# The left operands of the MLP's second half: one at a time through three products, with their sums on VectorE, instead of in packs of seven with their sums on GpSimd

## The chip, the cores and the metric

The kernel runs on one core of one Trainium2 chip. Five engines with queues of their own work side by side: TensorE (PE; PEld is its weight load), VectorE (DVE), ScalarE (ACT), GpSimd (POOL) and SyncE (SP), whose queue issues all transfers here. Each takes its instructions in order and waits for semaphores of the others. The metric is the device time of one execution in microseconds (us).

## The reference

One layer of a streaming encoder on 2048 positions with 1024 channels. A mixer (short convolution and retention) comes first; the change lies behind it, in the MLP:

```python
h = rms_norm(x, g_pre_mlp[layer]) * (1.0 + scale2) + shift2
f = jnp.square(jax.nn.relu(h @ w_fc1[layer])) @ w_fc2[layer]
x = x + gate2 * rms_norm(f, g_post_mlp[layer])
```

with `w_fc1` 1024 x 4096 and `w_fc2` 4096 x 1024, all in float32.

## The kernel before

**Products of three.** A float32 tile is split into a high part (ScalarE casts it to fp32r, line 806) and a low part (VectorE subtracts the high part from the tile, line 807). `mm3` makes one product from three matmuls (lines 142 to 144): high by high, low by high, high by low.

**Seven products for eight.** Each half of the positions (`B` = 0 and 1, 1024 positions) goes through both linear maps of the MLP by the Strassen-Winograd scheme: a 2x2 block product is made from seven products, numbered in the order 1, 2, 6, 7, 5, 3, 4, with sums of blocks on either side. The sequence is `fc1(0)`, `fc2(0)`, `fc1(1)`, `fc2(1)`.

**Left operands of fc1.** `h_left` makes them from the normalised activations in DRAM (`h2d`). For each of four packs p it loads four tiles a11, a12, a21, a22, makes four sums (s3 at line 842, and lines 847, 849, 851), and splits seven tiles (`sp_`), one per product. The splits stay in SBUF: qh and ql are their high and low parts. For B = 0 the work is done ahead of fc1(0). For B = 1 it is done beside fc2(0), with the engine for the sums handed over as `eng`.

**fc2 and its steps.** A product of fc2 is a loop over t = 0 to 15 (`prod`). Each step loads one tile `fw` of 128x1024, the activations (from `fd`) and the weights next to each other (line 964), splits both (fh and fl, wh and wl), and runs twelve matmuls, three for each of four PSUM banks. There are three buffers for fw, three each for wh and wl, ten for fh and fl together. So a load of fw for step t waits for wl of step t - 3, and a cast to wh waits for the matmuls of step t - 3.

**What sets the order.** The program is written in one sequence. A scheduler then places the instructions on each engine's queue, by priority and by its own model of times, so that work written later can stand earlier. `next(beside)` in `prod` says where in the written sequence a piece of `h_left` belongs.

Of the kernel before, what the change touches and what calls it, by code (L numbers as in the profile page):

```python
# [54 lines left out]
def block_kernel(  # L55
# [5 lines left out]
    nc = tc.nc  # L61
# [15 lines left out]
    def nm(s):  # L77
        n_of[s] = n_of.get(s, 0) + 1
        return f"{s}_{n_of[s]}"
# [108 lines left out]
    def mod1(kt):  # L188

        pt = st.tile([P, 256], F32, tag="pt", name=nm("pt"), bufs=4)  # L190
        for i in range(2):
            raw = st.tile([P, 4, 256], F32, tag="ada", name=nm("ada"), bufs=8)
            last = nc.sync.dma_start(raw, ada1[kt, i].rearrange("p (k c) -> p k c", k=4))
            for k in range(4):
                c_ = sc[:, 4 * i + k : 4 * i + k + 1]
                if i == k == 0:
                    nc.vector.tensor_scalar(pt, raw[:, k, :], c_, None, op0=ALU.mult)
                else:
                    nc.vector.scalar_tensor_tensor(  # L199
                        pt, raw[:, k, :], c_, pt, op0=ALU.mult, op1=ALU.add  # L200
                    )
        return pt, last
# [69 lines left out]
    with tc.tile_pool(name="st", bufs=NK) as st:  # L272
# [37 lines left out]
        pts, _ = mod1(0)  # L310
# [23 lines left out]
    def at(tag, shape=(P, 512), dt=F32, bufs=4):  # L334
        pool = {"yh": pl, "yl": pl, "kT": late, "sg": late}.get(tag, pa)
        return pool.tile(list(shape), dt, tag=tag, name=nm(tag), bufs=bufs)
# [156 lines left out]
    NP = DFF // P // 2  # L493
# [21 lines left out]
    with pa_stack:  # L515
# [30 lines left out]
        for b in range(NB):  # L546
# [36 lines left out]
            for ps in gemm_nat(w_in(GG), h_cur, KS):  # L583
                sg = at("sg")
# [5 lines left out]
            for t in range(NT):  # L590
# [3 lines left out]
                kT = at("kT")  # L594
# [195 lines left out]
    def q(n, tag):  # L790
        pool, t_ = late, tag
        if n % 2 == 0:
            pool, t_ = (pQ, tag) if tag == "junk" else (tp, {"kT": "tmpa", "sg": "tmpb"}[tag])
        return pool.tile([P, 512], F32, tag=t_, name=nm("q"), bufs=QB[tag])

    def r_():
        return h_("r", F32)

    def ld(src):
        a = r_()  # L800
        nc.sync.dma_start(a, src)
        return a

    def split512(src, tile_of):
        hi, lo = tile_of("h"), tile_of("l")
        nc.scalar.copy(hi, src)  # L806
        nc.vector.tensor_tensor(lo, src, hi.bitcast(F32), op=SUB)  # L807
        return hi, lo
# [10 lines left out]
    def left_tile(i):  # L819
        if i == 4:  # L820
            return lambda part: pQ.tile([P, 512], F32R, tag="four", name=nm("q" + part), bufs=8)
        return held(hA if i in (1, 2, 6) else hB)

    sd = {i: [dram.tile([P, 512], F32, name=f"sd{i}_{p}") for p in range(4)] for i in (7, 5, 3)}

    def h_left(B, res, eng, t2k, now):


        def sp_(i, a):
            if now or i not in sd:  # L830
                res[i].append(split512(a, left_tile(i)))
            else:
                nc.sync.dma_start(sd[i][len(sdn[i])], a)
                sdn[i].append(a)

        sdn = {i: [] for i in sd}
        for p in range(4):
            a11, a12, a21, a22 = (t2k(n) for n in range(4))
            for a, (i, j) in ((a11, (0, 0)), (a12, (0, 1)), (a21, (1, 0)), (a22, (1, 1))):
                nc.sync.dma_start(a, h2d[2 * B + i][2 * p + j])  # L840
            s3 = t2k(4)
            eng.tensor_tensor(s3, a11, a21, op=SUB)
            sp_(7, s3)
            sp_(1, a11)
            sp_(2, a12)
            sp_(4, a22)
            eng.tensor_tensor(a21, a21, a22, op=ADD)
            sp_(5, a21)
            eng.tensor_tensor(a11, a21, a11, op=SUB)
            sp_(6, a11)  # L850
            eng.tensor_tensor(a12, a12, a11, op=SUB)
            sp_(3, a12)
            yield
        if not now:
            for i in (7, 5, 3):
                for p in range(4):
                    res[i].append(split512(ld(sd[i][p]), left_tile(i)))
                yield

    def quads(t):  # L860
        return [ld(w1[t][:, i * 512 : i * 512 + 512]) for i in range(4)]
# [92 lines left out]
    def fc2(B, beside=None):  # L954
# [13 lines left out]

        def prod(i, bs, upto=NP, aside=None):
            for t in range(upto):  # L970
                if beside is not None and i in (1, 2) and t % 4 == 2:
                    next(beside, None)
                ah, al, bh, bl = operands(i, t)
                for n, ps in enumerate(bs):
                    s = slice(n * P, n * P + P)
                    mm3(ps, ah[:, s], al[:, s], bh, bl, t == 0, t == NP - 1)
                if aside is not None:
                    next(aside, None)
# [91 lines left out]

    hl = [{i: [] for i in ORDER} for _ in range(2)]
    left = h_left(0, hl[0], nc.vector, lambda n: r_(), False)
    for _ in range(4):
        next(left)
    fc1(0, hl[0], quads(0), left, mixer_end())
    tail = fc2(0, h_left(1, hl[1], nc.gpsimd, lambda n: q(1, "kT" if n < 4 else "sg"), True))
    fc1(1, hl[1], quads(0), None, tail)
    fc2(1)

# [83 lines left out]
```

## Time and profile before

| | us |
|---|---|
| median of 3 runs | 2254.37 (2247.35 to 2257.65) |
| the profiled execution | 2248.11 |
| its span, first to last instruction | 2246.30 |
| PE busy | 2146.0 (96%) |
| DVE busy | 1446.0 (64%) |
| ACT busy | 989.3 (44%) |
| POOL busy | 616.0 (27%) |

The page's chain of waits gives 64% of the span to PE, 12% to transfers, 7% to DVE and 5% to POOL. The busy shares are means over all stages. To see what one stage waits for, the span is cut into windows of time, and the rows of one engine are read in order of time with the idle time in front of each. A granted clock (PEclk) of 1.00 is TensorE's full 2.4 GHz.

### The profile page before, as it was taken

The numbers are of one execution on the slowest core, as the hardware profiler recorded it, in microseconds if no ns is written. First come the engines' busy times: TensorE is split into PE (matmuls) and PEld (weight loads), VectorE is DVE, ScalarE is ACT, GpSimd is POOL, SyncE is SP. The second block draws the span as 40 slices with busy tenths as digits, with TensorE's granted clock in tenths as the row PEclk, the third lists the DMA queues.
The fourth block names the chain that finished last, engine by engine and source line by source line (L and its number), as shares of the span: only waits on it lengthen the run. The fifth ranks groups of instructions, "written<-read, shape, count | busy, mean of one in ns | idle before, by whom it ended". The sixth has DMA issues, their size and how long they took to land.

```text
span 2246.3 us, 28437 instructions
## 1 busy us (share of the span) xinstructions
PE 2146.0 (96%) x9736; PEld 1769.4 (79%) x9736; DVE 1446.0 (64%) x2182; ACT 989.3 (44%) x1714; POOL 616.0 (27%) x457
## 2 busy tenths in 40 slices
PE   3999999999999999979999989999999999999997
PEld 2788877878787888868888867888888888888885
DVE  7766854774577535776666776656776666555566
ACT  3332533253224422565555554444445555454453
POOL 4133163305323442152333331101333333010012
PEclk8999999999999999999999999999999999999998
DMA  7456477446655563665444366666764443666656
GB/s 277 138 176 225 160 244 244 158 151 224 203 188 189 193 223 106 229 206 189 154 155 155 136 220 200 195 192 197 253 235 150 150 149 138 193 197 196 197 188 253
DMA packets 197426, 428.23 MB, mean 191 GB/s; under 512 B 22560, under 2 KB 22560, under 8 KB 197280
## 3 DMA queue, kind: packets, MB, share of 16 engines
q1 hardware_dynamic: 197280, 426.41, 57.5%
q8 instruction: 76, 1.25, 0.2%
q14 instruction: 70, 0.57, 0.1%
HBM read 322.51 MB, written 103.81 MB: 190 GB/s over the span
## 4 chain that ended last, share of the span: by engine, by line
PE 64%; DMA 12%; issue 11%; DVE 7%; POOL 5%; ACT 1%; SPq 1%; DVEq 0%; POOLq 0%; ACTq 0%
PE g L142 19%; PE g L144 19%; PE g L143 19%; DMA w2r<-in_w 3%; DMA w2d<-w2r 2%; POOL w2r L502 2%; PE m L142 2%; PE m L143 2%; PE m L144 2%; DMA ada<-in_ada 1%; DMA fw<-fd 1%; DMA x<-in_x 1%; DVE pt L199 1%; DVE ql L807 1%; DVE wl L807 1%
## 5 line engine op out<-in xcount | busy, mean ns | idle before, releaser
L143 PE MATMUL g<-ql,wh 128*128 128x512 f32 x896 | 350.0, 391 | 9.8 <-DVE ql L807 9.8
L144 PE MATMUL g<-qh,wl 128*128 128x512 f32 x896 | 350.2, 391 | 0.8 <-DVE wl L807 0.6
L142 PE MATMUL g<-qh,wh 128*128 128x512 f32 x896 | 349.4, 390 | 0.8 <-ACT wh L806 0.6
L136 ACT CAST whi<-raw 128x1024 fp32r<-128x1024 f32 x148 | 155.3, 1052 | 348.2 <-PE g L144 175.5
L864 DVE TENSOR_TENSOR q<-g,q 128x512 f32<-128x512 f32 x267 | 178.4, 687 | 174.3 <-PE g L144 174.1
L138 DVE TENSOR_TENSOR wlo<-raw,whi 128x1024 fp32r<-128x1024 f32 x140 | 188.9, 1353 | 151.1 <-ACT whi L136 150.7
L143 PE MATMUL g<-wl,fh 128*128 128x512 f32 x680 | 266.9, 392 | 8.9 <-DVE wl L807 8.8
L807 DVE TENSOR_TENSOR fl<-fw,fh 128x512 fp32r<-128x512 f32 x218 | 165.7, 761 | 170.1 <-ACT fh L806 168.9
L144 PE MATMUL g<-wh,fl 128*128 128x512 f32 x680 | 265.9, 391 | 0.0
L806 ACT CAST fh<-fw 128x512 fp32r<-128x512 f32 x218 | 135.2, 620 | 234.6 <-DMA fw<-fd 225.9
L806 ACT CAST wh<-r 128x512 fp32r<-128x512 f32 x224 | 138.8, 620 | 216.3 <-PE g L143 189.3
L142 PE MATMUL g<-wh,fh 128*128 128x512 f32 x680 | 219.8, 391 | 2.7 <-ACT wh L806 2.7
L143 PEld LDWEIGHTS g<-ql,wh 128*128 128x128 f32 x896 | 168.6, 188 | 46.2 <-DVE ql L807 11.6
L144 PEld LDWEIGHTS g<-qh,wl 128*128 128x128 f32 x896 | 168.7, 188 | 37.4 <-DVE wl L807 2.8
L142 PEld LDWEIGHTS g<-qh,wh 128*128 128x128 f32 x896 | 168.7, 188 | 36.5 <-ACT wh L806 0.8
L807 DVE TENSOR_TENSOR wl<-fw,wh 128x512 fp32r<-128x512 f32 x218 | 158.2, 727 | 45.4 <-ACT wh L806 45.1
L994 POOL TENSOR_TENSOR q<-q,gg 128x512 f32<-128x512 f32 x28 | 43.1, 1566 | 467.2 <-ACT q L991 342.0
L807 DVE TENSOR_TENSOR wl<-r,wh 128x512 fp32r<-128x512 f32 x224 | 164.1, 733 | 10.9 <-ACT wh L806 10.4
L806 ACT CAST wh<-fw 128x512 fp32r<-128x512 f32 x218 | 134.8, 619 | 65.5 <-PE g L144 31.3
L882 POOL TENSOR_TENSOR r<-r,r 128x512 f32<-128x512 f32 x32 | 42.4, 1325 | 429.0 <-DVE wl L807 388.8
L143 PEld LDWEIGHTS g<-wl,fh 128*128 128x128 f32 x680 | 128.5, 189 | 38.4 <-DVE wl L807 11.9
L142 PEld LDWEIGHTS g<-wh,fh 128*128 128x128 f32 x680 | 128.0, 189 | 30.5 <-ACT wh L806 3.9
(257 smaller groups left out, 4478.0 us busy)
## 6 DMA issues: line engine op xcount, KB each, us to landing
raw<-in_win SPq DMA_DIRECT2D x116, 512.0 KB, 4.2
fd<-q SPq DMA_DIRECT2D x224, 256.0 KB, 2.2
fw<-fd SPq DMA_DIRECT2D x224, 256.0 KB, 2.7
r<-in_w SPq DMA_DIRECT2D x128, 256.0 KB, 4.7
fw<-w2d SPq DMA_DIRECT2D x128, 256.0 KB, 3.0
ada<-in_ada SPq DMA_DIRECT2D x48, 512.0 KB, 4.7
fw<-in_w SPq DMA_DIRECT2D x96, 256.0 KB, 3.5
w2r<-in_w SPq DMA_DIRECT2D x32, 512.0 KB, 4.9
```

The costliest lines, as they stand in the source:

```text
L136: nc.scalar.copy(hi, raw)
L138: (eng or nc.vector).tensor_tensor(lo, raw, hi.bitcast(F32), op=ALU.subtract)
L142: nc.tensor.matmul(ps, ah, bh, start=first, stop=False)
L143: nc.tensor.matmul(ps, ah, bl, start=False, stop=False)
L144: nc.tensor.matmul(ps, al, bh, start=False, stop=last)
L199: nc.vector.scalar_tensor_tensor(pt, raw[:, k, :], c_, pt, op0=ALU.mult, op1=ALU.add)
L502: nc.gpsimd.tensor_tensor(o, a, b_, op=ALU.subtract)
L806: nc.scalar.copy(hi, src)
L807: nc.vector.tensor_tensor(lo, src, hi.bitcast(F32), op=SUB)
L864: (eng or nc.vector).tensor_tensor(o, a, b_, op=ADD)
L882: nc.gpsimd.tensor_tensor(b11, b12, b11, op=SUB)
L994: eng.tensor_tensor(c, c, gg[1][:, j * 512 : j * 512 + 512], op=ALU.mult)
```

## The change

For B = 1, `h_left` now hands back control after each split operand and no longer after a pack of seven. `prod` calls for the next one in products 1, 2 and 6, from the fifth step of product 1 on, 28 calls over 40 steps, where it called once every four steps of products 1 and 2. The sums of lines 842 to 851 (844 to 859 now) are made on VectorE (`nc.vector`) and no longer on GpSimd (`nc.gpsimd`). For B = 0 the 28 calls are made in one loop, as the four were.

```diff
+    LEFT = 28
+
     def h_left(B, res, eng, t2k, now):
...
             s3 = t2k(4)
             eng.tensor_tensor(s3, a11, a21, op=SUB)
             sp_(7, s3)
+            yield
             sp_(1, a11)
+            yield
             sp_(2, a12)
+            yield
             sp_(4, a22)
+            yield
             eng.tensor_tensor(a21, a21, a22, op=ADD)
             sp_(5, a21)
+            yield
             eng.tensor_tensor(a11, a21, a11, op=SUB)
             sp_(6, a11)
+            yield
             eng.tensor_tensor(a12, a12, a11, op=SUB)
             sp_(3, a12)
             yield
...
         def prod(i, bs, upto=NP, aside=None):
             for t in range(upto):
-                if beside is not None and i in (1, 2) and t % 4 == 2:
-                    next(beside, None)
+                if beside is not None and i in (1, 2, 6):
+
+                    k = (1, 2, 6).index(i) * NP + t - 4
+                    if k >= 0 and (k + 1) * LEFT // 40 > k * LEFT // 40:
+                        next(beside, None)
...
     left = h_left(0, hl[0], nc.vector, lambda n: r_(), False)
-    for _ in range(4):
+    for _ in range(LEFT):
         next(left)
     fc1(0, hl[0], quads(0), left, mixer_end())
-    tail = fc2(0, h_left(1, hl[1], nc.gpsimd, lambda n: q(1, "kT" if n < 4 else "sg"), True))
+    tail = fc2(0, h_left(1, hl[1], nc.vector, lambda n: q(1, "kT" if n < 4 else "sg"), True))
```

What the scheduler makes of it changes in one place of the program alone, steps 6 of product 1 to 8 of product 2 of fc2(0); ahead of it and behind it the kinds and the order of the instructions are the same on every engine. On VectorE, the first pack of left operands stood like this before (ql is a low part of a left operand, fl and wl those of the activations and weights of a step of fc2):

```order
L807 TENSOR_TENSOR ql_11328<-q_11325,qh_11327 128x512
L807 TENSOR_TENSOR fl_11518<-fw_11514,fh_11517 128x512
L807 TENSOR_TENSOR wl_11522<-fw_11514,wh_11521 128x512
L807 TENSOR_TENSOR ql_11345<-q_11319,qh_11344 128x512
L807 TENSOR_TENSOR fl_11541<-fw_11537,fh_11540 128x512
L807 TENSOR_TENSOR ql_11350<-q_11317,qh_11349 128x512
L807 TENSOR_TENSOR fl_11564<-fw_11560,fh_11563 128x512
L807 TENSOR_TENSOR wl_11545<-fw_11537,wh_11544 128x512
L807 TENSOR_TENSOR ql_11355<-q_11318,qh_11354 128x512
```

In the changed program the same pack stands like this, with the four sums (L844, L853, L856, L859) in VectorE's own queue:

```order
L807 TENSOR_TENSOR ql_11474<-q_11387,qh_11473 128x512
L844 TENSOR_TENSOR q_11394<-q_11386,q_11388 128x512
L807 TENSOR_TENSOR wl_11435<-fw_11427,wh_11434 128x512
L853 TENSOR_TENSOR q_11388<-q_11388,q_11389 128x512
L807 TENSOR_TENSOR ql_11501<-q_11389,qh_11500 128x512
L807 TENSOR_TENSOR ql_11397<-q_11394,qh_11396 128x512
L856 TENSOR_TENSOR q_11386<-q_11388,q_11386 128x512
L807 TENSOR_TENSOR fl_11454<-fw_11450,fh_11453 128x512
L807 TENSOR_TENSOR ql_11552<-q_11388,qh_11551 128x512
L807 TENSOR_TENSOR wl_11458<-fw_11450,wh_11457 128x512
L859 TENSOR_TENSOR q_11387<-q_11387,q_11386 128x512
L807 TENSOR_TENSOR fl_11481<-fw_11477,fh_11480 128x512
```

Sums and left splits now alternate with the splits of the steps. From the first left split to the last there were 55 VectorE rows (28 left splits, 14 fl, 13 wl); there are 80 now (28 left splits, 16 sums, 18 fl, 18 wl).

On SP, the loads of the second pack (q from h2d) stood between the loads of the steps (fw) like this before:

```order
L840 DMA q_11450<-h2d_2_639 128x512
L964 DMA fw_11624<-fd_1_10_8017 128x512
L964 DMA fw_11624<-in_w 128x512
L840 DMA q_11451<-h2d_3_640 128x512
L840 DMA q_11452<-h2d_2_647 128x512
L964 DMA fw_11647<-fd_1_11_8018 128x512
L964 DMA fw_11647<-in_w 128x512
L840 DMA q_11453<-h2d_3_648 128x512
```

and stand like this now:

```order
L842 DMA q_11657<-h2d_2_639 128x512
L842 DMA q_11658<-h2d_3_640 128x512
L972 DMA fw_11527<-fd_1_10_8017 128x512
L972 DMA fw_11527<-in_w 128x512
L842 DMA q_11659<-h2d_2_647 128x512
L972 DMA fw_11555<-fd_1_11_8018 128x512
L972 DMA fw_11555<-in_w 128x512
L842 DMA q_11660<-h2d_3_648 128x512
```

The second load has moved ahead of one step's loads; in the later packs each of the four stands by itself between the loads of two steps. Before, a load of h2d waited for a split on VectorE and, three times in four, for a sum on GpSimd; now it waits for a split on VectorE alone.

## Rows read from the trace of the kernel before

**Rows 1.** The page's first part, all engines: busy us, share of the span, instructions.

```profile
PE 2146.0 (96%) x9736; PEld 1769.4 (79%) x9736; DVE 1446.0 (64%) x2182; ACT 989.3 (44%) x1714; POOL 616.0 (27%) x457
```

**Rows 2.** Windows ahead of the stretch, of the stretch, and behind it: from:to, length, then busy us (instructions) of PE, PEld, DVE, ACT, POOL, then the granted clock, the share of the DMA engines and GB/s.

```profile
1270.00:1310.61 40.61, 40.61 (x180) 33.61 (x180) 29.31 (x42) 21.80 (x38) 6.54 (x4) 1.00 0.48 158
1310.61:1368.07 57.46, 46.45 (x182) 35.47 (x181) 47.56 (x57) 33.61 (x61) 25.05 (x16) 0.94 0.63 201
1380.00:1600.00 220.00, 220.00 (x972) 182.15 (x972) 134.58 (x200) 103.15 (x185) 21.81 (x16) 1.00 0.65 207
```

**Rows 3.** TensorE in order of time: start, us, what, and in brackets the idle time in front and what ended it. Line 142 is the first of the three matmuls and its first row the start of a step.

```profile
1310.61 0.61 PE L142 MATMUL g<-wh,fh 128*128 128x512 f32 x2
...
1313.33 0.61 PE L142 MATMUL g<-wh,fh 128*128 128x512 f32 x2
...
1316.05 1.07 PE L142 MATMUL g<-wh,fh 128*128 128x512 f32 x4
1319.16 0.80 PE L143 MATMUL g<-wl,fh 128*128 128x512 f32 x1 [2.04 <-DVE wl L807]
...
1321.04 0.63 PE L143 MATMUL g<-wl,fh 128*128 128x512 f32 x1
1321.46 0.63 PE L144 MATMUL g<-wh,fl 128*128 128x512 f32 x1
...
1368.07 0.62 PE L142 MATMUL g<-wh,fh 128*128 128x512 f32 x2
...
1371.41 0.73 PE L142 MATMUL g<-wh,fh 128*128 128x512 f32 x2 [0.46 <-ACT wh L806]
```

**Rows 4.** Windows of ten microseconds, columns as in rows 2.

```profile
1280.00:1290.00 10.00, 10.00 (x46) 8.27 (x45) 9.10 (x15) 5.28 (x9) 1.31 (x1) 1.00 0.36 134
...
1320.00:1330.00 10.00, 10.00 (x40) 8.12 (x40) 7.65 (x13) 4.61 (x8) 2.80 (x2) 0.88 0.79 244
1330.00:1340.00 10.00, 7.37 (x25) 5.28 (x24) 9.61 (x12) 5.78 (x11) 3.47 (x3) 0.83 0.66 208
```

**Rows 5.** Waits in the stretch 1310.61 to 1368.07 us: who waited for whom, us in all, times, longest.

```profile
ACT fh L806 <- DMA fw<-fd: 12.5, 5, 3.0
...
ACT qh L806 <- DMA q<-h2d: 9.7, 9, 1.9
PE g L143 <- DVE wl L807: 8.8, 5, 2.3
...
PE g L142 <- ACT wh L806: 2.2, 2, 1.7
```

**Rows 6.** GpSimd in order of time: the four sums of the first pack, and the last of the third.

```profile
1311.63 1.57 POOL L842 TENSOR_TENSOR q<-q,q 128x512 f32<-128x512 f32 x1 [30.31 <-DMA q<-h2d]
1313.27 1.30 POOL L847 TENSOR_TENSOR q<-q,q 128x512 f32<-128x512 f32 x1
1314.65 1.63 POOL L849 TENSOR_TENSOR q<-q,q 128x512 f32<-128x512 f32 x1
1316.35 1.60 POOL L851 TENSOR_TENSOR q<-q,q 128x512 f32<-128x512 f32 x1
...
1345.00 1.60 POOL L851 TENSOR_TENSOR q<-q,q 128x512 f32<-128x512 f32 x1
```

**Rows 7.** VectorE in order of time, at the same two places.

```profile
1309.50 0.69 DVE L807 TENSOR_TENSOR ql<-q,qh 128x512 fp32r<-128x512 f32 x1 [2.04 <-ACT qh L806]
1310.75 0.69 DVE L807 TENSOR_TENSOR ql<-q,qh 128x512 fp32r<-128x512 f32 x1 [0.56 <-ACT qh L806]
...
1316.75 1.76 DVE L807 TENSOR_TENSOR fl<-fw,fh 128x512 fp32r<-128x512 f32 x1
1318.43 0.68 DVE L807 TENSOR_TENSOR wl<-fw,wh 128x512 fp32r<-128x512 f32 x1
...
1345.39 1.75 DVE L807 TENSOR_TENSOR wl<-fw,wh 128x512 fp32r<-128x512 f32 x1
1347.07 0.68 DVE L807 TENSOR_TENSOR ql<-q,qh 128x512 fp32r<-128x512 f32 x1
1347.67 0.68 DVE L807 TENSOR_TENSOR fl<-fw,fh 128x512 fp32r<-128x512 f32 x1
```

**Rows 8.** Groups of instructions in the stretch, shapes kept apart: busy us, mean ns of one, and the idle time in front of them with what ended it.

```profile
L807 DVE TENSOR_TENSOR ql<-q,qh 128x512 fp32r<-128x512 f32 x27 | 23.9, 898 | 5.0 <-ACT qh L806 4.8
...
L806 ACT CAST qh<-q 128x512 fp32r<-128x512 f32 x27 | 16.4, 620 | 10.8 <-DMA q<-h2d 9.7 <-POOL q L849 0.6 <-POOL q L847 0.2
L807 DVE TENSOR_TENSOR fl<-fw,fh 128x512 fp32r<-128x512 f32 x15 | 14.6, 974 | 5.2 <-ACT fh L806 5.2
L807 DVE TENSOR_TENSOR wl<-fw,wh 128x512 fp32r<-128x512 f32 x15 | 12.4, 824 | 0.0
```

**Rows 9.** Transfers by line: KB each and the median time in us from issue to landing, in the stretch 1310.61 to 1368.07 us.

```profile
fw<-fd SPq DMA_DIRECT2D x15, 256.0 KB, 3.6
fw<-in_w SPq DMA_DIRECT2D x14, 256.0 KB, 4.3
q<-h2d SPq DMA_DIRECT2D x12, 256.0 KB, 3.6
```

**Rows 10.** The same behind it, from 1380 to 1500 us.

```profile
fw<-fd SPq DMA_DIRECT2D x45, 256.0 KB, 2.7
...
fw<-in_w SPq DMA_DIRECT2D x5, 256.0 KB, 3.1
```

## The prediction

> **What bounds the kernel now.** I read the busy shares first. TensorE is busy 96% of the span and VectorE 64% [rows 1]; so a change to the helpers can gain only where TensorE waits. Then I cut the span into windows until I found where it does. In the 40 us ahead of 1310.61 us, and again from 1380 us to 1600 us, TensorE is busy all the time at granted clock 1.00; between them lies one stretch of 57.46 us in which it is busy 46.45 us, at a mean clock of 0.94 [rows 2]. In that same stretch GpSimd is busy 25.05 us and VectorE 47.56 us, the highest share it has in any of these windows. The stretch is the second half of product 1 and the first steps of product 2 of the first fc2, and GpSimd does nothing there but the sums of the left operands.
>
> What the stretch costs follows from TensorE's own rows. A step of a product (one t: four banks, three matmuls each) begins every 2.72 us while nothing is late: 1310.61, 1313.33, 1316.05 [rows 3]. From 1310.61 to 1368.07 there are fifteen steps (t = 5 to 15 of product 1, t = 0 to 3 of product 2), 15 x 2.72 = 40.80 us of work in 57.46 us: 16.66 us lost. The first step after it loses 0.46 us more [rows 3]. So 17.1 us is all that the change can win here. It is not only idle time: for some microseconds after a gap the matmuls start 0.43 us apart [rows 3], not 2.72 / 12 = 0.227 us, and the windows with gaps show a granted clock of 0.88 and 0.83 [rows 4], between the levels of 2.4 GHz (1.00) and 1.2 GHz. This part goes with the gaps.
>
> The waits say who is late: TensorE waits for VectorE's low parts of the weights, wl, 8.8 us in five gaps of up to 2.3 us, and for a cast by ScalarE 2.2 us [rows 5]. VectorE is late for two reasons. Its subtractions take 0.68 us and start 0.60 us apart when GpSimd is still, as at 1347.07 and 1347.67, but 1.75 to 1.78 us while GpSimd runs a sum, as at 1316.75 and 1345.39 [rows 6, 7]; by groups their means are 0.898, 0.974 and 0.824 us [rows 8]. At a spacing of 0.602 us the 57 subtractions would take 34.3 us instead of 47.56 us, so some 13 us is lost beside GpSimd. And VectorE waits 10.2 us for casts (5.0 + 5.2) [rows 8], which themselves wait for transfers (12.5 and 9.7 us) [rows 5].
>
> The Trainium skill's page "SBUF — State Buffer" (Who interferes with whom) states a mechanism for the first: a VectorE instruction with two SBUF inputs and a GpSimd instruction that reads SBUF need the same read port, and the one that comes second waits until the first is done. The 1.76 us beside 0.68 us agree; by this rule the whole 13 us go when the sums leave GpSimd.
>
> **The change part by part.**
>
> *GpSimd's sixteen sums go to VectorE.* Removed: 25.05 us of GpSimd, with what it does to VectorE, about 13 us. Added: sixteen 128x512 operations on VectorE at 0.60 us from start to start, 9.6 us. Also removed: the chain of four dependent GpSimd sums per pack, 1311.63 to 1317.95 us in the first [rows 6], for which three splits and the reuse of the load buffers wait.
>
> *The order.* The code asks for one left operand in some 1.4 steps, over 40 steps. The scheduler does not keep that; it pulls the work ahead. In the order of the changed program the first left split still stands right after wl of t = 5, where it did, and the last stands 80 VectorE rows on: 28 left splits, 16 sums, and 36 splits of 18 steps. Before, the 28 left splits stood in 55 rows with 27 others, 13.5 steps. So VectorE's load per step falls: 80 x 0.602 = 48.2 us for 18 x 2.72 = 49.0 us of matmuls. It just fits, with under 1 us to spare. Before it was 47.56 us for 13.5 x 2.72 = 36.7 us, which could not fit.
>
> *Where it starts.* VectorE waits for the first loads of h2d as now (2.04 us ahead of 1309.50, 0.56 us ahead of 1310.75 [rows 7]). The next row is a sum that needs the third load, which GpSimd had at 1311.63 [rows 6]. Counting rows on from there, 0.60 us each, wl of t = 7 is done near 1317.2 us; TensorE wants it at 1316.05 + 4 x 0.227 = 1316.96. It came at 1319.1 [rows 7]. The wl of t = 8 is late by some 0.5 us, that of t = 10 early by 0.7, those of product 2 early by 0.7 to 2.5 us. With no wait on VectorE the stretch therefore costs 0.5 us, not 17.1.
>
> *Waits that stay.* VectorE takes its rows in order, so a cast that is late holds all behind it, and with a load of 98% what is lost is not made up. Loads take 3.6 to 4.3 us from issue to landing in this stretch, 2.7 to 3.1 us later [rows 9, 10]. In the new order a load of h2d is issued behind the row that frees its buffer and is wanted 7 to 11 rows on, 4.2 to 6.6 us; the activations' split fl stands 8 to 10 rows behind the wl that frees its buffer, before 5 to 8. Landing plus a cast of 0.62 us [rows 8] is 4.2 to 4.9 us: mostly covered, with some tenths missing here and there. Two loads a pack, four packs, some 0.4 us each: I take 3 us. The bounds are 0 (all covered) and the 10.2 us of now [rows 8]. I stay nearer the low end, since both the spacing and the load per step moved that way.
>
> *SP, ScalarE, transfers.* The SP queue has the same 16 loads, now one at a time between the loads of fw; each waits for one VectorE row, in the order in which VectorE runs them, so none blocks its queue for longer than VectorE itself lags. The waits on GpSimd's sums are gone. ScalarE has 64 casts and four copies in 18 steps, at the 33.61 us for 61 of now [rows 2] some 37.5 of 49 us: it hides. The bytes are the same. If the cover on ScalarE failed, it would show as late casts, the term above. The rest of the program keeps its order row for row, so nothing else moves.
>
> **The sum**, against the profiled execution (span 2246.30 us, 2248.11 us in all): -16.66 - 0.46 + 0.5 + 3.0 = -13.6 us, 2234.5 us. That execution lies 6.3 us under the median of the runs; on the median of 2254.37 us the same difference gives 2240.8, so 2241 us.
>
> **Rivals.**
>
> *The waits stay as they are.* If loads are issued as late as now against what needs them, VectorE still waits 10.2 us: -16.66 - 0.46 + 0.5 + 10.2 = -6.4 us, 2248 us. For it: landing is no shorter and the margin in rows is tenths. Against it: fl and the loads have more rows in between.
>
> *All of it goes.* Waits of 0: -16.6 us, 2238 us. For it: VectorE busy 9.1 us in 10 at 1280 to 1290 us left TensorE without a gap [rows 4]. Against it: that was short, and 98% over 49 us is not 91% over ten.
>
> *VectorE becomes the bound, slower than before.* If the long subtractions were not GpSimd's doing but that of the transfers or casts beside them, each VectorE row would keep its mean of 47.56 / 57 = 0.834 us; 80 rows take 66.7 us for 49.0 us of matmuls, 17.7 us late, and with 0.5 and 10.2 us of waits 28.4 us are lost instead of 17.1: +11.3 us, 2265.7 us. It turns to a loss from 0.78 us per row on (49.0 + 17.1 - 3.5 = 62.6 us over 80 rows). Against it: the long ones among the rows stand only where GpSimd runs [rows 6, 7]. The Trainium skill's page "Perfetto Trace Analysis" (Optimizing Scalar/DVE Operations) speaks for this rival: where VectorE is saturated, work may be taken off it, even to GpSimd. The same passage adds that the two share a port and the move might not help; the rows with 1.76 us agree with that second half.
>
> **How the numbers follow.** Forecast 0.54, all gone 0.20, waits as now 0.22, slower 0.04. The forecast's own range is 2236 to 2246. The range for 8 in 10 runs from 2233 (all gone, and a few us of scatter: the runs lie 2247.35 to 2257.65) to 2251 (waits as now, and the same scatter). A measurement of this kernel tells 0.5%, 11.3 us, from no change, so faster means below 2243.1: three quarters of the forecast, nearly all of the clean case and little of the waits, 0.63; slower by as much 0.03; the rest 0.34.
>
> **What would show it.** Right: no VectorE subtraction over 0.7 us between 1310 and 1360 us; TensorE with under 4 us of idle there and no window under a clock of 0.95; VectorE busy over nine tenths until near 1360 us, idle only for casts; product 2 of the first fc2 starting some 13 us earlier against the start of product 1. Wrong: 1.7 us operations without GpSimd beside them (the slower rival), or VectorE idle 8 us or more in front of splits whose casts wait for loads (the waits).

## The result, and the profile after

The changed kernel takes 2235.16 us (median of 6 runs, 2232.52 to 2240.46), the kernel before on the same chip 2252.42 us (6 runs, 2247.35 to 2257.65). The ratio is 0.9925, with a 95% interval of 0.9911 to 0.9939: faster by 17.3 us, by the interval 13.7 to 20.0 us. The forecast was a difference of 13.6 us and 2241 us, range 2233 to 2251. Of the 6 us between 2235.16 and 2241, 2 us come from the starting point: the forecast took the kernel before at 2254.37 us, the median of three runs.

The profiled execution is the slowest of the six (2240.46 us, span 2238.7 us). The page's first part beside [rows 1] shows little: POOL falls by 29.3 us and DVE by 3.2 us, though sixteen sums were added to it.

```profile
PE 2143.6 (96%) x9736; PEld 1765.9 (79%) x9736; DVE 1442.8 (64%) x2198; ACT 989.9 (44%) x1714; POOL 586.7 (26%) x441
```

The stretch of [rows 2] is to be found again. Step 5 of product 1 begins at 1316.46 us here and step 4 of product 2, fifteen steps on, at 1360.05 us. TensorE in order of time, the starts of some steps and the rows that have idle time in front of them:

```profile
1316.46 0.62 PE L142 MATMUL g<-wh,fh 128*128 128x512 f32 x2
...
1321.90 1.07 PE L142 MATMUL g<-wh,fh 128*128 128x512 f32 x4
1323.27 0.50 PE L143 MATMUL g<-wl,fh 128*128 128x512 f32 x1 [0.30 <-DVE wl L807]
...
1328.23 1.07 PE L142 MATMUL g<-wh,fh 128*128 128x512 f32 x4
...
1334.06 1.20 PE L142 MATMUL g<-wh,fh 128*128 128x512 f32 x4 [0.23 <-ACT wh L806]
...
1354.47 0.73 PE L142 MATMUL g<-wh,fh 128*128 128x512 f32 x2 [0.54 <-ACT wh L806]
...
1360.05 0.61 PE L142 MATMUL g<-wh,fh 128*128 128x512 f32 x2
```

The window between them (columns as in [rows 2]) and two of the ten-microsecond windows to set against [rows 4]:

```profile
1316.46:1360.07 43.61, 42.54 (x182) 33.28 (x181) 39.30 (x64) 30.43 (x56) 0.00 (x0) 1.00 0.83 262
```

```profile
1320.00:1330.00 10.00, 9.70 (x42) 7.40 (x41) 10.00 (x18) 7.14 (x13) 0.00 (x0) 1.00 0.80 247
1330.00:1340.00 10.00, 9.77 (x42) 7.37 (x42) 8.72 (x15) 7.27 (x14) 0.00 (x0) 1.00 0.83 267
```

43.59 us for 40.80 us of matmuls: 2.8 us are lost where 16.66 us were, 0.9 us of them in steps 7 and 8 of product 1 (1321.90 to 1328.23 us, 6.33 us for 5.44). The step after it now takes 2.72 us (1360.05 to 1362.77 us); before, it took 3.34 us (1368.07 to 1371.41 us [rows 3]) and so lost 0.62 us. The gain at this place is 14.5 us. GpSimd does nothing, the granted clock is 1.00 in these windows, and VectorE does 64 rows in 39.30 us, where 57 rows took 47.56 us. Row by row, at the place of [rows 7]:

```profile
1315.69 0.69 DVE L807 TENSOR_TENSOR ql<-q,qh 128x512 fp32r<-128x512 f32 x1 [2.07 <-ACT qh L806]
1316.97 0.69 DVE L807 TENSOR_TENSOR ql<-q,qh 128x512 fp32r<-128x512 f32 x1 [0.58 <-ACT qh L806]
1317.63 0.69 DVE L844 TENSOR_TENSOR q<-q,q 128x512 f32<-128x512 f32 x1
1318.24 0.69 DVE L807 TENSOR_TENSOR wl<-fw,wh 128x512 fp32r<-128x512 f32 x1
1318.91 0.69 DVE L853 TENSOR_TENSOR q<-q,q 128x512 f32<-128x512 f32 x1
```

The sums (L844, L853) stand in VectorE's queue as the order showed, and no row is longer than 0.69 us. The groups of the same window, and its waits:

```profile
L807 DVE TENSOR_TENSOR ql<-q,qh 128x512 fp32r<-128x512 f32 x22 | 14.3, 685 | 0.6 <-ACT qh L806 0.6
L807 DVE TENSOR_TENSOR wl<-fw,wh 128x512 fp32r<-128x512 f32 x15 | 10.3, 685 | 0.3 <-ACT wh L806 0.3
L807 DVE TENSOR_TENSOR fl<-fw,fh 128x512 fp32r<-128x512 f32 x14 | 9.6, 685 | 1.1 <-ACT fh L806 1.1
L844 DVE TENSOR_TENSOR q<-q,q 128x512 f32<-128x512 f32 x4 | 2.8, 689 | 0.2 <-DMA q<-h2d 0.2
L853 DVE TENSOR_TENSOR q<-q,q 128x512 f32<-128x512 f32 x3 | 2.1, 692 | 1.2 <-DMA q<-h2d 1.2
```

```profile
ACT fh L806 <- DMA fw<-fd: 6.8, 7, 2.5
ACT qh L806 <- DMA q<-h2d: 5.4, 6, 1.4
...
PEld g L143 <- DVE wl L807: 1.8, 4, 0.7
PEld g L142 <- ACT wh L806: 1.6, 2, 1.0
...
PE g L142 <- ACT wh L806: 0.8, 2, 0.5
```

The matmuls themselves show 1.1 us of idle time (0.3 for wl, 0.8 for wh); that more is lost shows in the weight loads (PEld), which wait for the same two. Means of 898, 974 and 824 ns [rows 8] are all 685 ns now. VectorE waits 3.4 us (0.6 + 0.3 + 1.1 + 0.2 + 1.2) where it waited 10.2 us, in part for loads of sums, which it did not have before. TensorE's wait of 8.8 us for wl [rows 5] is 0.3 us, and that is all that this group has in the whole program, as the page says:

```profile
L143 PE MATMUL g<-wl,fh 128*128 128x512 f32 x680 | 265.3, 390 | 0.3 <-DVE wl L807 0.3
```

### The profile page after: what moved, and what is told of

It reads as the page before. It is cut to its first block, busy times and chain, and to the rows that moved or that the text cites. A ratio compares the mean times of both kernels' runs of the same rounds, so it can differ in the third digit from the quotient of the medians.

```text
span 2238.7 us, 28424 instructions
## 1 busy us (share of the span) xinstructions
PE 2143.6 (96%) x9736; PEld 1765.9 (79%) x9736; DVE 1442.8 (64%) x2198; ACT 989.9 (44%) x1714; POOL 586.7 (26%) x441
## 4 chain that ended last, share of the span: by engine, by line
PE 67%; DMA 11%; issue 10%; DVE 7%; POOL 3%; ACT 1%; SPq 0%; DVEq 0%; POOLq 0%; ACTq 0%
PE g L142 20%; PE g L143 20%; PE g L144 20%; DMA w2r<-in_w 2%; DMA w2d<-w2r 2%; DMA fw<-fd 2%; PE m L142 2%; PE m L143 2%; PE m L144 2%; POOL w2r L502 2%; DMA ada<-in_ada 1%; DMA x<-in_x 1%; DVE pt L199 1%; DVE wl L807 1%; DVE ql L807 1%
## 5 line engine op out<-in xcount | busy, mean ns | idle before, releaser
L807 DVE TENSOR_TENSOR wl<-fw,wh 128x512 fp32r<-128x512 f32 x218 | 156.2, 717 | 44.7 <-ACT wh L806 42.2
L807 DVE TENSOR_TENSOR wl<-r,wh 128x512 fp32r<-128x512 f32 x224 | 163.6, 731 | 11.0 <-ACT wh L806 10.8
```

## A measure for the experiments

The programs start fc2(0) anywhere from 1297 to 1307 us in their profiled executions, also where all instructions ahead of it are the same. So the place is compared by itself: from TensorE's first matmul of fc2(0) to the first of product 7 lie products 1, 2 and 6, 48 steps. What exceeds 48 x 2.72 + 0.45 = 131.0 us is called the loss (0.45 us, because the row read for product 7 is that of its second bank pair, m, the name of these banks). Before, these are the rows:

```profile
1297.01 0.84 PE L142 MATMUL g<-wh,fh 128*128 128x512 f32 x3
...
1446.70 0.39 PE L142 MATMUL m<-wh,fh 128*128 128x512 f32 x1
```

and after:

```profile
1302.86 0.84 PE L142 MATMUL g<-wh,fh 128*128 128x512 f32 x3
...
1437.91 0.39 PE L142 MATMUL m<-wh,fh 128*128 128x512 f32 x1
```

149.69 and 135.05 us: losses of 18.7 and 4.0 us. Each loss comes from one profiled execution. What it varies by is seen where the same instructions ran twice or three times: 17.6 and 18.7 us, and 3.2 to 4.5 us. The medians of before in the four sets of runs are 2252.88, 2252.27, 2252.85 and 2251.4 us.

| kernel | GpSimd operations beside the left operands | median us | ratio, 95% interval | loss us |
|---|---|---|---|---|
| before | 16 sums | 2252.4 | 1 | 18.7 |
| after | none | 2235.16 | 0.9925 (0.9911 to 0.9939) | 4.0 |
| after_again | none | 2238.99 | 0.9945 (0.9930 to 0.9960) | 4.5 |
| vec_packs | none | 2236.08 | 0.9926 (0.9913 to 0.9939) | 3.2 |
| gps_ones | 16 sums | 2252.55 | 0.9995 (0.9986 to 1.0004) | 17.6 |
| paced_vec | none | 2243.22 | 0.9953 (0.9940 to 0.9966) | 7.3 |
| paced_gps | 16 sums | 2244.04 | 0.9962 (0.9949 to 0.9975) | 11.0 |
| paced_short | none | 2243.16 | 0.9960 (0.9947 to 0.9973) | 11.0 |
| gps_read | 16 that nobody uses | 2257.93 | 1.0021 (1.0011 to 1.0030) | 21.8 |
| gps_read2 | 8 that nobody uses | 2248.63 | 0.9984 (0.9971 to 0.9996) | 13.0 |
| gps_read1 | 4 that nobody uses | 2239.64 | 0.9956 (0.9939 to 0.9973) | 7.1 |
| gps_write | 48 fills | 2241.44 | 0.9948 (0.9935 to 0.9962) | 5.7 |
| half | 8 sums | 2249.78 | 0.9982 (0.9968 to 0.9995) | 15.6 |
| few_loads | none | 2240.15 | 0.9932 (0.9913 to 0.9950) | 4.8 |

## The experiments

Theory A is the prediction's: before lost what GpSimd's sums do to VectorE, and the scheduler sets the spacing. Theory B: the gain comes from asking for one operand at a time. Theory C: what counts is VectorE's time per step against the 2.72 us that a step lasts, by whatever rows.

### One half of the change at a time: the engine, the pacing

vec_packs is the kernel before with one word changed, and keeps the packs of seven:

```diff
-    tail = fc2(0, h_left(1, hl[1], nc.gpsimd, lambda n: q(1, "kT" if n < 4 else "sg"), True))
+    tail = fc2(0, h_left(1, hl[1], nc.vector, lambda n: q(1, "kT" if n < 4 else "sg"), True))
```

> The kernel before with one thing changed: the sums of the left operands on VectorE. The packs of seven stay as they were written. Theory A (the loss is what GpSimd's sums do to VectorE, and the scheduler sets the spacing by itself): the same as the changed kernel, some 2235 us, ratio 0.992 to 0.995, about 3 us lost in the stretch, no subtraction on VectorE over 0.7 us. Theory B (the gain comes from the operands being asked for one by one over three products): most of the gain is missing, 2245 to 2252 us.

gps_ones is the changed kernel with that word put back, so it has the pacing alone:

```diff
-    tail = fc2(0, h_left(1, hl[1], nc.vector, lambda n: q(1, "kT" if n < 4 else "sg"), True))
+    tail = fc2(0, h_left(1, hl[1], nc.gpsimd, lambda n: q(1, "kT" if n < 4 else "sg"), True))
```

> The other half of the change alone: operands asked for one by one through products 1, 2 and 6, the sums left on GpSimd. Theory A: no change against the kernel before, ratio within 0.3% of 1, some 17 us lost in the stretch, VectorE subtractions of 1.75 us beside GpSimd's sums. Theory B: most of the gain, 2238 us or less.

Measured: 2236.08 and 2252.55 us. The engine gives all of the gain, the pacing none. The built programs say why: apart from the numbers of lines and buffers, vec_packs has the instructions, the order and the waits of the changed kernel on all five engines, and gps_ones those of the kernel before. The scheduler moves the written places away. In gps_ones the gaps and the lower clock of [rows 4] are back:

```profile
1320.00:1330.00 10.00, 8.12 (x29) 6.24 (x28) 9.89 (x12) 6.52 (x13) 4.36 (x3) 0.83 0.62 199
...
1350.00:1360.00 10.00, 6.92 (x18) 5.20 (x19) 9.03 (x13) 5.45 (x10) 2.98 (x2) 0.68 0.57 171
```

Theory B falls. Since pacing alone changes no instruction, the two parts of the change are one: the engine moves the sums, and with them the scheduler's spacing (55 rows of VectorE in 13.5 steps become 80 in 18).

### The written pace, forced

To get the pace that the code asks for, each left operand's cast is tied behind the last cast of the step in which it is asked for:

```diff
-            if now or i not in sd:
+            if now:
+                step = cast["last"]
+                with tc.issue_after(step.ins):
+                    res[i].append(split512(a, left_tile(i)))
+                cast["last"] = step
+            elif i not in sd:
```

paced_vec is the changed kernel with this, paced_gps has the sums on GpSimd besides. In paced_vec 28 left splits and 16 sums now lie among 37 steps (118 of the 122 VectorE rows from the first left split to the last; the other four belong to the results of product 2).

> The changed kernel, with the pace now forced: the cast of each left operand is queued on ScalarE behind the cast of the step beside which it is written, so that the 28 operands really spread over some 37 steps. Theory C (what counts is VectorE's load per step against the 2.72 us of a step's matmuls): 122 VectorE rows x 0.602 = 73 us for 37 x 2.72 = 101 us, so no step is late: under 1 us lost where the changed kernel lost about 3, some 2 us less than that kernel, 2233 us. Rival (the loads of h2d are what is late, whatever the load): 3 us lost as in the changed kernel.

> The forced pace, with the sums on GpSimd. Theory C: 106 VectorE rows x 0.602 = 64 us and 13 us for the rows that GpSimd's sixteen sums lengthen, 77 us for 101 us of matmuls: hardly a step is late although the long subtractions are all there, under 3 us lost, 2234 to 2238 us. Theory A taken strictly (each sum on GpSimd costs TensorE its time, wherever it stands): 10 us or more lost, 2245 us or more.

Measured: 2243.22 and 2244.04 us. Both miss theory C. On this chip vec_packs, with the instructions of the changed kernel, took 2236.08 us; paced_vec, forecast below that, took 7.1 us more, and lost 7.3 us where under 1 us was expected. The windows of the two kernels behind the end of product 2, when its results are taken from the banks beside the first steps of product 6, first paced_vec, then the changed kernel:

```profile
1400.00:1410.00 10.00, 7.92 (x34) 5.90 (x34) 9.97 (x12) 6.87 (x16) 6.49 (x4) 1.00 0.43 134
```

```profile
1400.00:1410.00 10.00, 10.00 (x45) 8.28 (x45) 7.07 (x9) 4.57 (x8) 2.11 (x2) 1.00 0.62 196
```

In paced_vec VectorE is full, with twelve rows in 9.97 us, 0.83 us each: left splits, the splits of the steps and the additions of product 2. Beside them GpSimd does four multiplications by the gain, 6.49 us, and the long VectorE rows are back. TensorE waits for wl there:

```profile
1405.05 1.77 DVE L807 TENSOR_TENSOR ql<-q,qh 128x512 fp32r<-128x512 f32 x1
1406.74 1.77 DVE L807 TENSOR_TENSOR fl<-fw,fh 128x512 fp32r<-128x512 f32 x1
```

```profile
1405.18 0.50 PE L143 MATMUL g<-wl,fh 128*128 128x512 f32 x1 [1.10 <-DVE wl L807]
...
1409.17 0.50 PE L143 MATMUL g<-wl,fh 128*128 128x512 f32 x1 [0.98 <-DVE wl L807]
```

The changed kernel makes no left operands there, and loses nothing.

The two forced kernels also answer each other. Their code differs only in the engine of the sums, and they take 2244.04 against 2243.22 us, with intervals that overlap, and lose 11.0 against 7.3 us, where the same sums make 14.6 us in the unforced order. At a pace that leaves VectorE time, what GpSimd takes from it costs the program much less. Theory A taken strictly has its 10 us by the loss, but 7.3 us of them are there without any such sum.

What stands behind product 2 is 2 us of paced_vec's miss and not the whole, so paced_short takes the pace away from that place: 28 operands over 22 steps, done before product 2 ends.

```diff
-                    if k >= 0 and (k + 1) * LEFT // 40 > k * LEFT // 40:
-                        next(beside, None)
+                    if k >= 0:
+                        for _ in range((k + 1) * LEFT // 22 - k * LEFT // 22):
+                            next(beside, None)
```

> The forced pace of before, sums on VectorE, but the 28 operands spread over 22 steps, from step 4 of product 1 to step 10 of product 2, so that none is made at the end of product 2, where GpSimd multiplies by the gain. VectorE has 28 + 22 + 22 + 16 = 88 rows in 22 steps, at 0.60 us from start to start 53 us of 60 us. Theory C (the load per step, and at the end of product 2 GpSimd's multiplications beside it, made the wide pace lose): no step waits by more than 0.5 us, the two products lose under 2.5 us against 4.0 of the changed kernel, and the time is 2231 to 2237 us, not above that of the changed kernel on the same chip by more than 1 us. If the forcing itself (casts queued behind those of the right operands) is what costs: 2239 us or more, with steps that wait for VectorE all along product 1.

Measured: 2243.16 us, and 2238.99 us for the changed kernel on the same chip. The forecast by theory C is wrong and its rival right: the forcing costs, though at 0.60 us a row VectorE has time to spare. The loss is 11.0 us. VectorE is in the middle of it not full but idle:

```profile
1330.00:1340.00 10.00, 8.96 (x37) 6.60 (x36) 6.80 (x12) 5.45 (x10) 0.00 (x0) 1.00 0.66 221
```

```profile
1337.63 0.69 DVE L860 TENSOR_TENSOR q<-q,q 128x512 f32<-128x512 f32 x1 [3.11 <-DMA q<-h2d]
```

Transfers of this kernel from 1330 to 1338 us, KB each and median time from issue to landing:

```profile
fw<-fd SPq DMA_DIRECT2D x3, 256.0 KB, 6.1
...
q<-h2d SPq DMA_DIRECT2D x1, 256.0 KB, 6.5
```

A sum (L860) stands 3.11 us at the head of VectorE's queue, waiting for a load of h2d that took 6.5 us to land. It is this bunch that is slow and not the whole stretch: the median of the loads of h2d is 4.1 us here (1318 to 1381 us) as in the changed kernel (1305 to 1362 us). Eight loads were issued close together, between 1328.94 and 1333.71 us, and the next one of fw at 1340.15 us: the loads wait for buffers that VectorE frees, and VectorE, held by the sum, frees none. The dearer place of this kind comes later. Seven loads are issued between 1361.23 and 1364.08 us, the next one at 1367.34 us, and a cast for a step waits for its load:

```profile
1369.40 0.62 ACT L806 CAST fh<-fw 128x512 fp32r<-128x512 f32 x1 [2.89 <-DMA fw<-fd]
```

Steps 4 and 5 of product 2 lose 3.8 of the 11.0 us there. So the even pace has its price in loads, which bunch, and in rows that wait for them at the head of a queue and hold the splits of the steps behind them. That the bunching comes from the forced casts alone is argued from these rows, not shown by a run of its own.

> The changed kernel itself beside the three others on one chip: 2233 to 2239 us, by its six runs so far.

Measured: 2238.99 us (2235.93 to 2245.79). Its median is at the upper end of what was expected; three of its six runs lie above 2239 us.

### What does GpSimd take from VectorE, and by what?

gps_read keeps the sums on VectorE and puts GpSimd back beside them, with work that nobody waits for (spare is a buffer that was free, gg[1] the gain):

```diff
+                nc.gpsimd.tensor_tensor(spare, a22, gg[1][:, 0:512], op=SUB)
+                for _ in range(3):
+                    nc.gpsimd.tensor_tensor(spare, spare, gg[1][:, 0:512], op=SUB)
```

> The changed kernel (sums on VectorE) with four GpSimd subtractions 128x512 per pack of seven put back beside them; they read the same buffers in SBUF and their result is used by nobody, so nothing waits for them. Theory A (VectorE is slowed while GpSimd does a two-input operation): VectorE's rows beside them go from 0.69 us to some 1.7 us, GpSimd's from 1.2 to 1.6 us; four packs with four rows of about 1.6 us each slow VectorE for some 26 us, in which it does what 10 us hold otherwise, so up to 13 us come back: 2243 to 2251 us, products 1 and 2 losing 8 us or more. Theory C (only the number of rows per step on VectorE against a step's 2.72 us counts, and what GpSimd does is nothing to it): the time stays at 2233 to 2239 us.

gps_write has GpSimd busy at the same places and as long (27 us, in gps_read 25 us), but reading next to nothing:

```diff
+                nc.gpsimd.tensor_tensor(spare[:, 0:1], a22[:, 0:1], gg[1][:, 0:1], op=SUB)
+                for _ in range(12):
+                    nc.gpsimd.memset(spare, 0.0)
```

> The same places as in the run before, but what GpSimd does there reads next to nothing: one subtraction of a single column and twelve fills of 128x512 per pack, which only write. If it is GpSimd's reading of two operands that slows VectorE: VectorE's rows stay at 0.69 us and the time at 2233 to 2240 us. If any work of GpSimd in SBUF does it: rows of over 1 us as in the run before, and 2243 us or more.

Measured: 2257.93 us, slower than the kernel before and 7 us above theory A's range, and 2241.44 us, which its interval does not set apart from the changed kernel on the same chip (2238.99 us). The scheduler moved the rows a little: from the first left split to the last there are 80 rows in 18 steps, as in the changed kernel, but some stand in another order. gps_read, gps_write and the two kernels of the next section, gps_read2 and gps_read1, have one and the same order on VectorE, ScalarE and SP, so these four are compared with one another. VectorE in gps_read, in order of time, and GpSimd in the same microseconds:

```profile
1323.63 1.78 DVE L858 TENSOR_TENSOR q<-q,q 128x512 f32<-128x512 f32 x1
1325.33 1.76 DVE L807 TENSOR_TENSOR fl<-fw,fh 128x512 fp32r<-128x512 f32 x1
1327.01 1.75 DVE L807 TENSOR_TENSOR ql<-q,qh 128x512 fp32r<-128x512 f32 x1
1328.69 0.68 DVE L861 TENSOR_TENSOR q<-q,q 128x512 f32<-128x512 f32 x1
```

```profile
1323.24 4.98 POOL L848 TENSOR_TENSOR q<-q,gg 128x512 f32<-128x512 f32 x3
```

Three GpSimd rows in 4.98 us, and beside them three VectorE rows of 1.75 to 1.78 us, starting 1.69 us apart instead of 0.60: one for one, each GpSimd subtraction takes 1.09 us from VectorE. Sixteen of them are 17.4 us, where theory A had counted up to 13 us. The next row, with GpSimd still again, is at 0.68 us. In gps_write, the same four rows of the order, and GpSimd's fills in the same microseconds:

```profile
1317.04 0.69 DVE L858 TENSOR_TENSOR q<-q,q 128x512 f32<-128x512 f32 x1
1317.64 0.68 DVE L807 TENSOR_TENSOR fl<-fw,fh 128x512 fp32r<-128x512 f32 x1
1318.25 0.68 DVE L807 TENSOR_TENSOR ql<-q,qh 128x512 fp32r<-128x512 f32 x1
1318.85 0.68 DVE L861 TENSOR_TENSOR q<-q,q 128x512 f32<-128x512 f32 x1
```

```profile
1316.16 6.95 POOL L848 MEMSET q<- 128x512 f32 x12
```

Twelve fills back to back, and VectorE's rows stay at 0.68 us. So it is not GpSimd being busy, nor its writing, and not the transfers or the casts, which stand in the same order in both kernels. What is left is its reading of operands; a fill is another instruction as well, and no run has GpSimd read with a third one. The Trainium skill's page "SBUF — State Buffer" (Who interferes with whom) says just this: a VectorE instruction with two inputs in SBUF contends with a GpSimd instruction that reads SBUF, and not with one that only writes it. The rows agree on both halves, with 1.76 and 0.68 us.

A row of paced_vec bears on VectorE's side. Its addition of a PSUM bank (m) to a tile in SBUF, beside GpSimd's second multiplication by the gain, is not lengthened, where rows with two tiles of SBUF took 1.77 us. It is a single row, and no run tests it:

```profile
1403.36 0.68 DVE L879 TENSOR_TENSOR q<-m,q 128x512 f32<-128x512 f32 x1
```

### How the loss grows with GpSimd's operations

half puts two of the four real sums of each pack back on GpSimd, the last two:

```diff
-            eng.tensor_tensor(a11, a21, a11, op=SUB)
+            (nc.gpsimd if now else eng).tensor_tensor(a11, a21, a11, op=SUB)
...
-            eng.tensor_tensor(a12, a12, a11, op=SUB)
+            (nc.gpsimd if now else eng).tensor_tensor(a12, a12, a11, op=SUB)
```

> The changed kernel with two of the four sums of each pack (the last two, which hang on one another) back on GpSimd: 8 of 16. Theory A (each sum on GpSimd costs what it takes from VectorE beside it, about 1 us, so the loss grows with their count): the stretch loses about half of what before lost over the change, 5 to 10 us in the two products, and the time is 2240 to 2248 us, some 8 us above the changed kernel. Theory D (before lost because a pack's chain sum to cast to split to step ran at GpSimd's slow pace, so that the last, chained sums are what counts): with these on GpSimd the time is that of before within 3 us, 2249 us or more.

Measured: 2249.78 us (2243.91 to 2253.28) and a loss of 15.6 us, nearly all of before with half of its sums. By the number theory D has it. But half differs in a second way: with fewer rows on VectorE the scheduler puts the 28 left splits closer, 65 rows in 14.5 steps. The next two runs keep the order of gps_read and vary the count alone; gps_read2 has gps_read's loop once, and gps_read1 not at all:

```diff
-                for _ in range(3):
+                for _ in range(1):
```

> The useless GpSimd subtractions again, but two per pack instead of four: 8 in all, with every other instruction of the changed kernel in its order (80 rows of VectorE in 18 steps). Load theory (what counts is VectorE's time in those steps: 80 rows at 0.60 us are 48.2 us, and each GpSimd subtraction beside it adds about 1 us, against 18 steps of 2.72 us, 49.0 us): 48.2 + 8 = 56 us, 7 us more than the steps have, and with the 3 to 4 us that the changed kernel loses anyway the two products lose 9 to 12 us: 2243 to 2248 us, half way between the changed kernel and the run with sixteen. Chain theory (a GpSimd operation costs only where its own result is waited for): no change, 2233 to 2240 us.

> The same with one useless subtraction per pack, 4 in all. Load theory: 48.2 + 4 = 52 us of VectorE for 49.0 us of steps, 3 us more than there is, so the two products lose 6 to 8 us and the time is 2239 to 2244 us. Chain theory: no change, 2233 to 2240 us.

Measured: 2248.63 and 2239.64 us, losses of 13.0 and 7.1 us; the first lies a little above the range of the load theory, the second within it, but by its time alone within the chain theory's too. In this one order, with no such subtraction (gps_write), 4, 8 and 16, the loss is 5.7, 7.1, 13.0 and 21.8 us: about 1 us for each over all sixteen (16.1 us), although nobody waits for their results. The first four add only 1.4 us, hardly more than two executions of one program differ by. The changed kernel's own order loses 3.9 us on the mean (after, after_again, vec_packs). The group of GpSimd and one of VectorE in gps_read2:

```profile
L848 POOL TENSOR_TENSOR q<-q,gg 128x512 f32<-128x512 f32 x4 | 6.5, 1620 | 0.3
```

```profile
L858 DVE TENSOR_TENSOR q<-q,q 128x512 f32<-128x512 f32 x4 | 4.9, 1236 | 0.6 <-DMA q<-h2d 0.6
```

The chain theory falls for these subtractions: eight that nobody waits for make 13.0 us. So theory D is not needed for most of half's loss. What half's number comes from shows in an account of VectorE's time in the steps that hold the 28 left splits: rows x 0.602 us, 1.09 us for each GpSimd operation, against steps x 2.72 us, and 3.9 us that are lost anyway:

| order | rows, steps | VectorE us | steps us | too much + 3.9 | measured loss |
|---|---|---|---|---|---|
| before | 55, 13.5 | 33.1 + 17.4 | 36.7 | 17.7 | 18.7 |
| half | 65, 14.5 | 39.1 + 8.7 | 39.4 | 12.3 | 15.6 |
| after | 80, 18 | 48.2 | 49.0 | 3.9 | 3.2 to 4.5 |
| gps_read1 | 80, 18 | 48.2 + 4.4 | 49.0 | 7.5 | 7.1 |
| gps_read2 | 80, 18 | 48.2 + 8.7 | 49.0 | 11.8 | 13.0 |
| gps_read | 80, 18 | 48.2 + 17.4 | 49.0 | 20.5 | 21.8 |

The account carries all but 1.3 us of five kernels, and of half all but 3.3 us, which no run settles; the wait for the chained sums may have its part there. With gps_write's 5.7 us, the loss of their own order, in place of 3.9 us the last three rows come to 9.3, 13.6 and 22.4 us, and the account holds to 2.2 us. It does not hold for the forced kernels (paced_short: 82 rows in 19 steps, 49.4 of 51.7 us, and a loss of 11.0 us): it leaves out waits for loads, which stand in that kernel's rows.

### What holds the last microseconds

few_loads leaves out the loads of the last three packs, which use the first pack's blocks again:

```diff
-            a11, a12, a21, a22 = (t2k(n) for n in range(4))
+            if p == 0 or not now:
+                a11, a12, a21, a22 = (t2k(n) for n in range(4))
...
-                nc.sync.dma_start(a, h2d[2 * B + i][2 * p + j])
+                if p == 0 or not now:
+                    nc.sync.dma_start(a, h2d[2 * B + i][2 * p + j])
```

> The changed kernel without 12 of the 16 loads that feed the left operands: the blocks of the first pack are used again for the other three, so their operands are not those of the reference; sums, casts and splits are all there. It is to tell what the 2 to 4 us are that the changed kernel still loses in these two products. If transfers that land late hold them (16 blocks more on a queue that is busy for 80 per cent of the time): they lose under 1.5 us, and the time is 2231 to 2236 us. If VectorE's own load holds them (its rows here: 75 in 16 steps, at 0.60 us 45 us of 43.5 us): 2 us or more are still lost, with steps that wait for the split of a right operand while VectorE is busy, 2235 to 2240 us.

Measured: 2240.15 us (2239.09 to 2240.82), loss 4.8 us; taking the loads away gave nothing back. VectorE is full there from 1320 to 1350 us, and TensorE waits for it at once:

```profile
1320.00:1330.00 10.00, 7.02 (x30) 5.18 (x29) 10.00 (x18) 7.25 (x14) 0.00 (x0) 1.00 0.34 106
```

```profile
1323.24 0.50 PE L143 MATMUL g<-wl,fh 128*128 128x512 f32 x1 [1.79 <-DVE wl L807]
```

That speaks for VectorE's load, in this order (75 rows in 15.5 steps, 45.2 of 42.2 us). For the changed kernel's own order it settles less: without the loads the scheduler put the rows closer, so the one limit was relaxed and the other tightened. By the account above 3.0 of the 4.8 us are VectorE's excess, which leaves 1.8 us where the changed kernel loses 3.9 us; that points to the loads for a part of these. In the changed kernel itself 0.9 of its 2.8 us in the stretch are lost in steps 7 and 8 of product 1, with a wait for wl, and 1.9 us later, where TensorE's idle time ends with casts of wh on ScalarE; whether loads or ScalarE's other work make these late, no run tells apart. That VectorE's load and the loads from DRAM both have a part is argued from this and not shown.

## Why the prediction was right, point by point

- **Where the time is lost.** The forecast let nothing change outside the stretch. Measured between the first matmul of fc2(0) and product 7 the gain is 14.6 us (149.69 - 135.05), in the stretch and the step after it 14.5 us; the forecast was 13.6 us. Right, but for one reading: 0.46 us is only the idle time at the end of the step after the stretch [rows 3]; that step took 3.34 us and so lost 0.62 us.
- **VectorE at 0.60 us a row.** Right: means of 685 ns for the splits and 682 to 692 ns for the sums, no row above 0.7 us; and gps_read against gps_write show that the long rows were the doing of GpSimd's reads.
- **The walk and the waits that stay, 0.5 + 3.0 us.** 2.8 us measured in the stretch, so the sum of the two is right; each by itself is off, in opposite ways. The walk from the first sum on, with no wait on VectorE, cost 0.9 us (steps 7 and 8) and not 0.5; what came later cost 1.9 us and not 3.0. VectorE's waits are 3.4 us in the window, near the 3.0 us that were taken between the bounds of 0 and 10.2; but they did not all add up to lateness, for some of them fell where TensorE had splits in stock, as at 1346.27 us (0.76 us for a load), around which TensorE has no gap. That the choice of 3.0 us came out so near is in part luck: it was a guess between the bounds.
- **The order.** Right, and more than was said: the written pacing has no effect at all on the program, and the spacing comes with the engine.
- **The rival that is slower.** It rested on VectorE's rows staying long without GpSimd. There is no such row. The price that it put on long rows was of the right kind: gps_read, where the sums are on VectorE and the reads of GpSimd beside them, is slower than the kernel before.
- **The rivals of more and of less.** By the median of the runs, the 16.6 us of "all of it goes" are nearer to the 17.3 us than the forecast is. Its condition did not come true: VectorE still waits 3.4 us, and 2.8 us are still lost. Nor did that of "the waits stay as they are", 10.2 us.
- **The signs named.** The windows' clock (1.00) and TensorE's idle time there (1.1 us by busy time) came as said. VectorE is busy 39.30 of 43.61 us, nine tenths, but not in each window (8.57 to 10.00). Product 2 was to start some 13 us earlier against the start of product 1; it starts 10.8 us earlier (56.55 to 45.72 us), because 3.8 us of the gain lie in products 2 and 6. That sign set the whole gain into the first product, though [rows 2] has its stretch run four steps into the second.
- **The total.** The median fell by 17.3 us, 3.7 us more than forecast. The same instructions gave 16.8 us in vec_packs and 13.3 us in after_again, so the forecast of 13.6 us stands at the low end of these, and the median of 2235.16 us lies just below the forecast's own range of 2236 to 2246 us. Whether 14.6 us, as these two traces have it, or some 16 us is the truth is left open: the time ahead of fc2(0) alone varies by up to 10 us between profiled executions.

## What to carry to other kernels

Before a helper engine is given work, count the busy engine's time in the stretch where its results are wanted: rows times their spacing, plus what the helper's reads take from it, against the matmuls of that stretch. A GpSimd subtraction of 128x512 with two operands cost VectorE 1.09 us here, more than the 0.60 us that VectorE takes to make one itself; it cost the program that much only where VectorE had no time left. And compare the built order before reading an effect into a source line: half of this change altered no instruction, and forcing its pace cost 4 to 7 us.

## What had not been expected

- GpSimd and VectorE took turns one row each: three of GpSimd's beside three of VectorE's, 1.69 us from start to start. GpSimd paid as well: 1.60 to 1.62 us for a subtraction beside VectorE's, 1.30 us in the row that has least beside it [rows 6].
- Twelve GpSimd fills of 128x512 in 6.95 us left VectorE's subtractions at 0.68 us.
- The scheduler answered a change of engine with another spacing (13.5, 14.5 and 18 steps for 16, 8 and 0 sums on GpSimd), and with half of the sums on GpSimd 11.6 us (15.6 - 4.0) of the 14.6 us of all were lost.
